# GpSimd's weight low parts in eight instructions, negated maxima on ScalarE, and an earlier window pair and key block, in a hybrid transformer layer on Trainium2

## The chip, the cores and the metric

The kernel runs on one core of one Trainium2 chip. The metric is the device time in microseconds of one execution. A core has five engines that run their own instruction streams and meet at semaphores: TensorE (PE in the profile, with its weight loads shown as PEld), VectorE (DVE), ScalarE (ACT), GpSimd (POOL) and SyncE (SP), which here only issues DMA transfers. Operands lie in on-chip memory (SBUF), matrix products land in PSUM, and everything else is in device memory (DRAM).

## The reference

One layer of a bidirectional trunk: 1024 tokens of width 1024, in three sub-layers. Each of them norms its input, and its normed output is added to the residual.

```python
# 1. mixer: one input projection, then
#    (A) window attention, +-128 tokens, 8 query heads, 2 key/value heads
#    (B) gated delta rule in both directions, 4 heads, chunked
m = jnp.maximum(jnp.max(scores, axis=-1, keepdims=True), sk)      # (A), sk is a sink logit
p = jnp.exp(scores - m)
denom = jnp.sum(p, axis=-1, keepdims=True) + jnp.exp(sk - m)
o = jnp.einsum('bnhgqk,bnkhd->bnqhgd', p / denom, vw)
...
def step(state, inp):                                             # (B), over the chunks
    v_new = u_i - jnp.einsum('bhck,bhkv->bhcv', w_i, state)
    o_i = jnp.einsum('bhck,bhkv->bhcv', qg_i, state) + jnp.einsum('bhij,bhjv->bhiv', qk_i, v_new)
    state = state * gl_i[..., None, None] + jnp.einsum('bhck,bhcv->bhkv', kg_i, v_new)
#    both outputs side by side, times w_out
# 2. cross attention: 4 heads of 256, queries from the tokens (w_cq),
#    keys and values from 256 memory tokens (w_ckv), times w_co
# 3. SwiGLU feed-forward of width 2816
```

## The kernel before

**Products in two parts.** Every float32 operand of a large product is split in a high part, which TensorE takes at full rate, and a low part, which is the rest; a product is then three products (high by high, high by low, low by high). The helper `split` (lines 100 to 106) makes the two: ScalarE copies the source into the high part (line 103), and VectorE, or GpSimd if it is named, subtracts (line 104). Weights go through `load_w` (lines 117 to 129): a 512 KB DMA on SP's queue into `wraw` (line 125), then `split` into `whi` and `wlo`, all from a pool with two buffers each. A weight tile is 128 partitions by 1024 elements, seen as 8 blocks of 128 (`k` = 8) or 2 blocks of 512.

Two callers ask `load_w` for the low part on GpSimd: `next_keys` (lines 976 to 987, a key block: 8 tiles of `w_ckv`, one for each block of 128 columns, 24 products each at line 984 that take `whi` and `wlo` one block of 128 at a time) and `cross_q` (line 1178 on, 16 tiles of `w_cq`, 24 products each at line 276 into `pcq`). Another 12 weight tiles of the feed-forward part have their low part on GpSimd by a call of `split` of their own.

**The middle stage.** Between the input projection (until about 285 us) and the product with `w_out` (from about 536 us) run three kinds of work that don't depend on one another:

- window attention, 16 windows (8 blocks of tokens by 2 key/value heads), by the generator `window` (lines 664 to 722): scores (line 685), scaled and banded scores with their row maximum by VectorE into `sc` and `m4` (line 687), the maximum negated into `nm` (line 692), four exponentials with `nm` as bias on ScalarE (line 694), the sum `es` with the sink (GpSimd 697, ScalarE 698, VectorE 699 and 700), four normalisations (VectorE at 703, ScalarE at 705 for five windows), then transposes (712), a split (`ph`, `pl`), the product with the values (717) and the store into `d_mix`. `next_windows` starts two of them.
- the scan of the gated delta rule by the generator `scan` (lines 825 to 944), 8 steps of four stages for each of two groups. A step is a chain of TensorE products (line 844) and VectorE or ScalarE copies: `kv` (872), `vg` (879), `vn` (881), the state `S` (889 and 892), the outputs `of` and `ol` (900 to 905). In the second half of the steps a gate is applied (919 to 931) and `late` turns, scales (`osq`, line 938) and stores the output into `d_mix` (line 941, SP's queue).
- the cross attention's memory: `memory_norm`, eight `next_keys` and two `next_values`.

The program order of these comes from a list of tokens, `ORDER_3` (line 39), worked off by `issue`: `M` is the memory's norm, `W` a pair of windows, `K` a key block, `V` a half of the values, and `s01` one step of both scans. A scheduler then sets the order on each engine from this program order, from the priorities (`load_w` has a raised one) and from costs of its own. `marks` holds an instruction of each window; the splits of `d_mix` (lines 1147 to 1150), which feed the product with `w_out` at line 1105 (`pmg`), may not be issued ahead of the one of window 14. The first `w_out` tiles go through `load_w` with the low part on VectorE.

Of the kernel before, what the change touches and what calls it, by code (L numbers as in the profile page):

```python
# [14 lines left out]
ALU = mybir.AluOpType  # L15
# [20 lines left out]

ORDER_1 = ("k0 k1 E0 K0 U0 E1 K1 U1 S0 q0 v0 q1 C0 v1 E2 C1 k2 E3 k3 q2 K2 U2 v2 K3 U3 S1 q3 C2 v3 C3 B0 B1").split()
ORDER_2 = "L0 L1 A4 V A0 A1 G0 G1 L2 L3 W W W A2 A3 G2 G3 W".split()
ORDER_3 = ("M s01 W K s01 W K s01 W s01 W K s01 W s01 K K s01 K K K s01 V V s01").split()


_NAMES = ["ident", "mUi", "mLi", "m5", "m6", "band0", "band1", "band2", "mU", "mL", "ones"]
# [34 lines left out]
def tile_hybrid_block(  # L77
# [4 lines left out]
    g_ffn_pre, w_gate_up, w_down, g_ffn_post, consts, out, dump=None, stop=None,  # L82
):
    nc = tc.nc
    x, mem, out = x[0], mem[0], out[0]
# [8 lines left out]
    def f32(ap):  # L94
        return ap.bitcast(F32)
# [4 lines left out]
    def split(hi, lo, src, scale=None, eng=None):  # L100

        if scale is None:
            nc.scalar.copy(hi, src)  # L103
            return (eng or nc.vector).tensor_tensor(lo, src, f32(hi), ALU.subtract)  # L104
        nc.scalar.activation(hi, src, AF.Identity, scale=scale)
        return nc.vector.scalar_tensor_tensor(lo, src, scale, f32(hi), ALU.mult, ALU.subtract)
# [11 lines left out]
    def load_w(src, k, n, eng=None, after=None, place=None):  # L118

        with tc.high_priority(AHEAD):  # L120
            raw = place or wp.tile([P, k, n], F32, tag="wraw", name="wraw")
            with ExitStack() as order_:
                if after:
                    order_.enter_context(tc.issue_after(after.ins))
                nc.sync.dma_start(raw, src.rearrange("(k p) n -> p k n", p=P))
            hi = wp.tile([P, k, n], F32R, tag="whi", name="whi")
            lo = wp.tile([P, k, n], F32R, tag="wlo", name="wlo")
            split(hi, lo, raw, eng=eng)
        return hi, lo


# [47 lines left out]
    sink = prm[:, 16:24]  # L179
# [43 lines left out]
    for hf in range(2):  # L223
        hi = hx.tile([P, KT, HALF], F32R, name=f"hhi{hf}")
        lo = hx.tile([P, KT, HALF], F32R, name=f"hlo{hf}")
# [10 lines left out]
        for k in range(KT):  # L236
# [3 lines left out]
            g = gcol[:, k:k + 1]  # L240
# [89 lines left out]
    for hf in range(2):  # L330
        pp = pg.tile([P, 512], F32, tag="pg", name="pg")
# [331 lines left out]
    def window(n, g):  # L663

        tok = slice(n * P, (n + 1) * P)
        k0, k1 = max(n - 1, 0), min(n + 1, NT - 1) + 1
        nb = k1 - k0
        w = nb * P
        band = C[:, _AT["band0"] - C0 + (k0 - n + 1) * P:][:, 0:w]

        khi, klo = (t[:, k0 * P:k1 * P] for t in keys[g])
        qr = tw.tile([P, 4, P], F32, tag="qr", name="qr", bufs=1)
        for r in range(2):
            nc.sync.dma_start(qr[64 * r:64 * r + 64], d_q[256 * g:256 * g + 256, tok].rearrange("(h e) t -> e h t", h=4))
        qs = tw.tile([P, 4, P], F32R, tag="qs", name="qs")
        nc.scalar.copy(qs, qr)
        nc.gpsimd.tensor_tensor(qs[64:128], qr[64:128], f32(qs[64:128]), ALU.subtract)

        m4 = tw.tile([P, 4], F32, tag="m4", name="m4")
        ssum = tw.tile([P, 4], F32, tag="ssum", name="ssum")  # L680
        pr = []
        for hh in range(4):
            pp = pw.tile([P, 512], F32, tag="pw", name="psw")
            for i, kk in enumerate((khi, klo)):
                nc.tensor.matmul(pp[:, 0:w], qs[:, hh, :], kk, start=(i == 0), stop=(i == 1))
            sc = tw.tile([P, 384], F32, tag="sc", name="sc", bufs=8)
            nc.vector.tensor_tensor_reduce(out=sc[:, 0:w], in0=pp[:, 0:w], in1=band, scale=0.125,
                                           scalar=sink[:, 4 * g + hh:4 * g + hh + 1], op0=ALU.add, op1=ALU.max,
                                           accum_out=m4[:, hh:hh + 1])
            pr.append(sc)  # L690
        nm = tw.tile([P, 4], F32, tag="nm", name="nm")
        turned_round = nc.vector.tensor_scalar(nm, m4, -1.0, None, ALU.mult)
        for hh in range(4):
            nc.scalar.activation(pr[hh][:, 0:w], pr[hh][:, 0:w], AF.Exp, bias=nm[:, hh:hh + 1],
                                 accum_out=ssum[:, hh:hh + 1])
        es = tw.tile([P, 4], F32, tag="es", name="es")
        nc.gpsimd.tensor_tensor(es, sink[:, 4 * g:4 * g + 4], m4, ALU.subtract)
        nc.scalar.activation(es, es, AF.Exp)
        nc.vector.tensor_tensor(es, es, ssum, ALU.add)
        nc.vector.reciprocal(es, es)  # L700
        for hh in range(4):
            if not 8 <= g * NT + n < 13:
                nc.vector.tensor_scalar(pr[hh][:, 0:w], pr[hh][:, 0:w], es[:, hh:hh + 1], None, ALU.mult)
            else:
                nc.scalar.mul(pr[hh][:, 0:w], pr[hh][:, 0:w], es[:, hh:hh + 1])
        marks.append(turned_round)
        yield
        po = pw.tile([P, 4, P], F32, tag="pow", name="pow", bufs=1)
        for j in range(nb):
            pp = pw.tile([P, 512], F32, tag="pw", name="ptw")  # L710
            for hh in range(4):
                nc.tensor.transpose(pp[:, hh * P:(hh + 1) * P], pr[hh][:, j * P:(j + 1) * P], ident)
            ph = tw.tile([P, 512], F32R, tag="ph", name="ph")
            pl = tw.tile([P, 512], F32R, tag="pl", name="pl")
            split(ph, pl, pp)
            for i, pe_ in enumerate((ph, pl)):
                nc.tensor.matmul(po.rearrange("p h t -> p (h t)"), vhl[:, k0 + j, g].rearrange("p r e -> p (r e)"), pe_,
                                 start=(j == 0 and i == 0), stop=(j == nb - 1 and i == 1))
        ao = tw.tile([P, 4, P], F32, tag="ao", name="ao", bufs=1)[0:64]
        nc.scalar.copy(ao, po[64:128])  # L720
        nc.vector.tensor_tensor(ao, po[0:64], ao, ALU.add)
        nc.gpsimd.dma_start(d_mix[g * 256:(g + 1) * 256, tok].rearrange("(h e) t -> e h t", e=64), ao)
# [25 lines left out]
    wins, wins_done, marks = [], [0], []  # L748
# [12 lines left out]
    def issue(order, table):  # L761
        for o in order:
            table[o[0]](*(int(c) for c in o[1:]))
# [245 lines left out]
    def scan_step(pairs):  # L1009

        for _ in range(4):
            for s_ in pairs:
                next(s_, None)

    issue(ORDER_3, {"s": lambda *gs: scan_step([scans[g] for g in gs]), "W": next_windows, "M": memory_norm,
                    "K": next_keys, "V": next_values})
# [126 lines left out]
    for hf in range(2):  # L1143
        for kp in range(4):
            k2 = slice(2 * kp, 2 * kp + 2)
            raw = raws[hf]
# [23 lines left out]
    raw = LR2.enter_context(pool("raw2", 1, side="right")).tile([P, KT, HALF], F32, name="oraw")  # L1170
# [363 lines left out]
    for e in range(EARLY):  # L1534
        f = 2 * e
        w, A = [], []
# [358 lines left out]
```

## Time and profile before

| | |
|---|---|
| median of 3 runs | 1502.69 us |
| the runs | 1501.88, 1502.69 and 1506.23 us |
| profiled execution, its own time | 1504.28 us |
| its span in the trace | 1502.6 us |
| mean granted clock of TensorE | 0.996 of full speed |
| low parts on GpSimd (line 104) | 36, of them 24 by `load_w` |

The span is the stretch from the first to the last recorded instruction; 1.68 us of the execution's time lie around it. A row of the timeline gives the start, the duration, the engine, the line, the operation, the tiles (output, arrow, inputs), shapes, a count, and in square brackets the idle time of that engine just before it with what ended it. A row of the windows view gives a stretch of time, its length, the busy time of PE, PEld, DVE, ACT and POOL in it (with the number of instructions), the granted clock, the busy share of the DMA engines and their rate. A row of the chain of waits gives the start and duration of a piece of the chain of work that ended last.

### The profile page before, as it was taken

The numbers are of one execution on the slowest core, as the hardware profiler recorded it, in microseconds if no ns is written. First come the engines' busy times: TensorE is split into PE (matmuls) and PEld (weight loads), VectorE is DVE, ScalarE is ACT, GpSimd is POOL, SyncE is SP. The second block draws the span as 40 slices with busy tenths as digits, with TensorE's granted clock in tenths as the row PEclk, the third lists the DMA queues.
The fourth block names the chain that finished last, engine by engine and source line by source line (L and its number), as shares of the span: only waits on it lengthen the run. The fifth ranks groups of instructions, "written<-read, shape, count | busy, mean of one in ns | idle before, by whom it ended". The sixth has DMA issues, their size and how long they took to land.

```text
span 1502.6 us, 21339 instructions
## 1 busy us (share of the span) xinstructions
PE 1469.4 (98%) x7437; PEld 1239.6 (82%) x7437; DVE 1109.3 (74%) x1805; ACT 776.2 (52%) x1600; POOL 372.6 (25%) x410
## 2 busy tenths in 40 slices
PE   7999999999999999999999999999999999999998
PEld 6888877888889878888888877888888888888787
DVE  5878998577997866528767887676867764696666
ACT  7678844568467664555654774323223232444533
POOL 0011231442246203242201002343433342000030
PEclk9999999999999999999999999999999999999999
DMA  6244554656996585444855553443533433953355
GB/s 204 71 118 135 138 174 121 174 152 207 317 322 209 155 314 196 153 156 149 275 181 202 182 197 112 127 133 112 165 118 117 140 106 105 350 182 99 105 180 170
DMA packets 254168, 256.35 MB, mean 171 GB/s; under 512 B 18128, under 2 KB 186221, under 8 KB 254061
## 3 DMA queue, kind: packets, MB, share of 16 engines
q1 hardware_dynamic: 252141, 250.80, 52.7%
q0 software_dynamic: 768, 2.10, 0.5%
q10 hardware_dynamic: 1152, 2.10, 0.4%
q8 instruction: 58, 0.95, 0.3%
q14 instruction: 49, 0.40, 0.1%
HBM read 178.63 MB, written 73.70 MB: 168 GB/s over the span
## 4 chain that ended last, share of the span: by engine, by line
PE 68%; DVE 10%; DMA 4%; ACT 4%; issue 3%; SPq 1%; POOL 0%; DVEq 0%; ACTq 0%; POOLq 0%
PE pE L1511 7%; PE pD L1511 7%; PE pmg L1105 6%; PE pcq L276 6%; PE pdX L1733 6%; PE pA L1511 5%; PE pst L1324 5%; PE pB L1511 3%; PE pg L276 3%; PE psc L844 3%; PE pdA L1733 2%; PE pdD L1733 2%; PE pcs L1195 2%; PE pco L1222 1%; PE pck L984 1%
## 5 line engine op out<-in xcount | busy, mean ns | idle before, releaser
L103 ACT CAST whi<-wraw 128x1024 fp32r<-128x1024 f32 x96 | 100.6, 1049 | 123.3 <-DMA wraw<-in_w_gate_up_dram 39.5
L276 PE MATMUL pg<-hlo,whi 128*128 128x512 f32 x352 | 141.0, 401 | 0.0
L276 PE MATMUL pg<-hhi,whi 128*128 128x512 f32 x352 | 140.5, 399 | 0.0
L276 PE MATMUL pg<-hhi,wlo 128*128 128x512 f32 x352 | 140.2, 398 | 0.0
L104 POOL TENSOR_TENSOR wlo<-wraw,whi 128x1024 fp32r<-128x1024 f32 x36 | 88.0, 2444 | 175.8 <-ACT whi L103 163.7
L1511 PE MATMUL pA<-b,whi 128*128 128x512 f32 x352 | 109.8, 393 | 1.9 <-ACT whi L103 1.0
L104 DVE TENSOR_TENSOR wlo<-wraw,whi 128x1024 fp32r<-128x1024 f32 x60 | 74.1, 1235 | 36.1 <-ACT whi L103 31.8
L1511 PEld LDWEIGHTS pA<-b,whi 128*128 128x128 f32 x352 | 65.2, 188 | 17.1 <-ACT whi L103 1.9
L276 PEld LDWEIGHTS pg<-hhi,whi 128*128 128x128 f32 x352 | 67.3, 191 | 13.6 <-ACT hhi L241 0.3
L276 PEld LDWEIGHTS pg<-hhi,wlo 128*128 128x128 f32 x352 | 67.2, 191 | 12.6
L276 PEld LDWEIGHTS pg<-hlo,whi 128*128 128x128 f32 x352 | 67.0, 190 | 12.7
L1733 PE MATMUL pdX<-dhl,whi 128*128 128x512 f32 x264 | 76.1, 390 | 0.9 <-ACT dhl L103 0.7
L1603 POOL TENSOR_TENSOR act<-act,up 128x512 f32<-128x512 f32 x33 | 50.3, 1524 | 88.6 <-DVE up L1602 66.9
L103 ACT CAST whi<-araw 128x1024 fp32r<-128x1024 f32 (+1 forms) x36 | 35.3, 981 | 68.3 <-PE pdX L1733 27.5
L1511 PE MATMUL pA<-b,wlo 128*128 128x512 f32 x176 | 69.0, 392 | 0.5 <-DVE wlo L104 0.5
L104 DVE TENSOR_TENSOR wlo<-araw,whi 128x1024 fp32r<-128x1024 f32 (+1 forms) x36 | 40.7, 1132 | 34.2 <-ACT whi L103 34.1
L1574 POOL TENSOR_TENSOR sr<-wraw 128x512 f32<-128x512 f32 x22 | 29.9, 1357 | 139.8 <-DMA wraw<-in_w_gate_up_dram 86.4
L301 DVE SCALAR_TENSOR_TENSOR acc<-cp,cols,acc 128x1024 f32<-128x1024 f32 x48 | 63.0, 1315 | 0.2
L1733 PEld LDWEIGHTS pdX<-dhl,whi 128*128 128x128 f32 x264 | 49.3, 188 | 12.1 <-ACT dhl L103 1.1
L103 ACT CAST dhl<-b 128x512 fp32r<-128x512 f32 x66 | 40.3, 620 | 31.2 <-PE pdA L1733 13.2
L1575 DVE TENSOR_TENSOR sr<-sr,wraw 128x512 f32<-128x512 f32 x22 | 36.6, 1664 | 26.6 <-POOL sr L1574 26.6
L103 ACT CAST s0h<-sr 128x512 fp32r<-128x512 f32 x22 | 13.7, 622 | 79.3 <-POOL sr L1574 78.9
(504 smaller groups left out, 4330.2 us busy)
## 6 DMA issues: line engine op xcount, KB each, us to landing
wraw<-in_w_gate_up_dram SPq DMA_DIRECT2D x54, 512.0 KB, 3.8
kv<-d_kv SPq DMA_DIRECT2D x32, 512.0 KB, 6.2
wraw<-in_w_in_dram SPq DMA_DIRECT2D x22, 512.0 KB, 4.1
b<-in_w_down_dram SPq DMA_DIRECT2D x20, 512.0 KB, 6.5
araw<-d_as SPq DMA_DIRECT2D x20, 512.0 KB, 3.8
pz<-d_pz SPq DMA_DIRECT2D x32, 256.0 KB, 6.3
wraw<-in_w_ckv_dram SPq DMA_DIRECT2D x16, 512.0 KB, 7.1
wraw<-in_w_out_dram SPq DMA_DIRECT2D x16, 512.0 KB, 4.1
```

Of the source, the lines that this page charges most:

```text
L103: nc.scalar.copy(hi, src)
L104: return (eng or nc.vector).tensor_tensor(lo, src, f32(hi), ALU.subtract)
L276: nc.tensor.matmul(p_, w[:, k, :], ah[a][:, k, :], start=(k == 0 and i == 0), stop=(k == nk - 1 and i == 2))
L301: nc.vector.scalar_tensor_tensor(acc, cp[:, t:t + S], taps[t], acc, ALU.mult, ALU.add)
L844: nc.tensor.matmul(out[:, d, h, :], lt[:, d, h, :], rt[:, d, h, :], start=True, stop=True)
L1105: nc.tensor.matmul(pp[t], act[a][:, k, tt], w_[:, kk, :], start=(k == 0 and i == 0), stop=(k == KT - 1 and i == 2))
L1195: nc.tensor.matmul(pp[:, t2_, :], q[a][:, ct, tt], kr_[b_][:, ct, :], start=(j == 0 and i == 0), stop=(j == 1 and i == 2))
L1324: nc.tensor.matmul(bank, a[:, tt], w, start=(start and i == 0), stop=(stop and i == 2), skip_group_check=not check)
L1511: nc.tensor.matmul(out_, w[a][:, k, :], xx[b_][:, k, :], start=(start and k == 0 and i == 0), stop=(k == HK - 1 and i == 2), skip_group_ch ...
L1575: nc.vector.tensor_tensor(s[1], s[0], a_[:, 0:HK], ALU.subtract)
L1603: nc.gpsimd.tensor_tensor(o_, o_, up, ALU.mult)
L1733: nc.tensor.matmul(banks[t], a[:, k - k0, tt], w, start=(first and k == 0 and i == 0), stop=(k == NB - 1 and i == 2), skip_group_check=not ...
```

## The change

It has three parts. `load_w` with an engine named no longer calls `split`: ScalarE's copy stays one instruction, and the low part becomes eight instructions of 128 by 128 on GpSimd (24 tiles; the 12 of the feed-forward part stay whole). The negated maximum `nm` moves from VectorE to ScalarE, and `marks` holds the last maximum of a window in its place. `ORDER_3` is another: the first pair of windows and the first key block stand ahead of the first scan step, which is then followed by the second one at once, and one of the three key blocks ahead of the eighth step has moved ahead of the pair of windows before the sixth.

```diff
-ORDER_3 = ("M s01 W K s01 W K s01 W s01 W K s01 W s01 K K s01 K K K s01 V V s01").split()
+ORDER_3 = ("M W K s01 s01 W K s01 W s01 W K s01 K W s01 K K s01 K K s01 V V s01").split()
...
-            split(hi, lo, raw, eng=eng)
+            if eng is None:
+                split(hi, lo, raw)
+            else:
+                nc.scalar.copy(hi, raw)
+                for j in range(0, k, 1):
+                    js = slice(j, j + 1)
+                    eng.tensor_tensor(lo[:, js], raw[:, js], f32(hi[:, js]), ALU.subtract)
...
-            nc.vector.tensor_tensor_reduce(out=sc[:, 0:w], in0=pp[:, 0:w], in1=band, scale=0.125,
-                                           scalar=sink[:, 4 * g + hh:4 * g + hh + 1], op0=ALU.add, op1=ALU.max,
-                                           accum_out=m4[:, hh:hh + 1])
+            largest = nc.vector.tensor_tensor_reduce(out=sc[:, 0:w], in0=pp[:, 0:w], in1=band, scale=0.125,
+                                                     scalar=sink[:, 4 * g + hh:4 * g + hh + 1], op0=ALU.add,
+                                                     op1=ALU.max, accum_out=m4[:, hh:hh + 1])
...
-        turned_round = nc.vector.tensor_scalar(nm, m4, -1.0, None, ALU.mult)
+        nc.scalar.mul(nm, m4, -1.0)
...
-        marks.append(turned_round)
+        marks.append(largest)
```

The scheduled order changes with it, from the end of the input projection to the end of the cross attention; the feed-forward part stays as it was. Three places of it follow, by engine, with the line, the operation, the output, an arrow and the inputs. Lines of the changed kernel are six higher than those of before from `load_w` on (line 134 is the new subtraction).

On GpSimd, at the first two key blocks, this is the order before:

```order
L677 TENSOR_TENSOR qs<-qr,qs 64x512
L697 TENSOR_TENSOR es<-prm,m_3468 128x4
L104 TENSOR_TENSOR wlo<-wraw,whi 128x1024
L722 DMA d_mix<-ao 64x4x128
L677 TENSOR_TENSOR qs<-qr,qs 64x512
```

and this is the order now:

```order
L683 TENSOR_TENSOR qs<-qr,qs 64x512
L703 TENSOR_TENSOR es<-prm,m_3468 128x4
L134 TENSOR_TENSOR wlo<-wraw,whi 128x128 x8
L728 DMA d_mix<-ao 64x4x128
L683 TENSOR_TENSOR qs<-qr,qs 64x512
```

The eight small subtractions stand back to back in the place of the large one, with nothing of GpSimd's own between them.

On TensorE, where the scan begins (`psc` are the scan's products, `ptm` the transposes of the memory, `pck` the products of a key block, `psw` and `ptw` the windows' scores and transposes), before:

```order
L969 MATMUL ptm<-ident,mt 128x128 x16
L844 MATMUL psc<-kv,pz 128x128 x3
L685 MATMUL psw<-khi,qs 128x384
L685 MATMUL psw<-klo,qs 128x384
L844 MATMUL psc<-kv,pz 128x128
L712 MATMUL ptw<-ident,sc 128x128 x8
L844 MATMUL psc<-kv,pz 128x128 x2
```

and now:

```order
L691 MATMUL psw<-klo,qs 128x384
L990 MATMUL pck<-mT_4077,whi 128x256
L990 MATMUL pck<-mT_4078,whi 128x256
L850 MATMUL psc<-kv,pz 128x128 x8
L990 MATMUL pck<-mT_4077,wlo 128x256
L990 MATMUL pck<-mT_4077,whi 128x256
```

The first products of the scan have moved behind the start of the first key block, whose other products now lie between them and the next ones of the scan.

On VectorE, at the end of the scans (`osq` is the last output of a group's scan, the rows with `psw` and `m_5099` or `m_5113` are the row maxima of the last window, the last `wlo` is the low part of the first `w_out` tile, those ahead of it are of the values' weights), before:

```order
L703 TENSOR_SCALAR sc<-sc,es 128x384 x4
L938 SCALAR_TENSOR_TENSOR osq<-psc,cols,gate 128x512
L104 TENSOR_TENSOR wlo<-wraw,whi 128x1024
L104 TENSOR_TENSOR pl<-ptw,ph 128x512
L104 TENSOR_TENSOR wlo<-wraw,whi 128x1024
L104 TENSOR_TENSOR pl<-ptw,ph 128x512
L104 TENSOR_TENSOR wlo<-wraw,whi 128x1024
L687 ISA sc,m_5099<-psw,C,prm 128x256
```

and now:

```order
L944 SCALAR_TENSOR_TENSOR osq<-psc,cols,gate 128x512
L693 ISA sc,m_5113<-psw,C,prm 128x256
L693 ISA m_5113 128x1
L104 TENSOR_TENSOR wlo<-wraw,whi 128x1024
L727 TENSOR_TENSOR ao<-pow,ao 64x512
L693 ISA sc,m_5113<-psw,C,prm 128x256
L693 ISA m_5113 128x1
L104 TENSOR_TENSOR wlo<-wraw,whi 128x1024
L693 ISA sc,m_5113<-psw,C,prm 128x256
L693 ISA m_5113 128x1
L104 TENSOR_TENSOR wlo<-wraw,whi 128x1024
```

The last output of the scan no longer stands behind the four normalisations of a window, and all four maxima of the last window (the first of them is just above these rows) stand ahead of `w_out`'s first low part instead of behind it. On SP's queue the load of the first `w_out` tile comes behind two stores of `osq` now, with a load of the values' weights ahead of these, where it came behind four; and the load of the second `w_out` tile comes behind four loads of `d_mix`, where it came behind one.

## The prediction

> **What bounds the kernel now.** I read the page first: the span, the busy times and the shares of the chain that ended last.
>
> ```profile
> span 1502.6 us, 21339 instructions
> PE 1469.4 (98%) x7437; PEld 1239.6 (82%) x7437; DVE 1109.3 (74%) x1805; ACT 776.2 (52%) x1600; POOL 372.6 (25%) x410
> PE 68%; DVE 10%; DMA 4%; ACT 4%; issue 3%; SPq 1%; POOL 0%; DVEq 0%; ACTq 0%; POOLq 0%
> ```
>
> TensorE is busy for 1469.4 of 1502.6 us, and the change removes no product. Only its gaps can be won or widened. Where they lie in the changed part is told by the windows view in stretches of 50 us:
>
> ```profile
> 350.00:400.00 50.00, 46.89 (x336) 42.75 (x336) 39.90 (x104) 34.89 (x81) 12.92 (x15) 1.00 0.90 285
> 400.00:450.00 50.00, 48.35 (x383) 45.67 (x383) 48.12 (x132) 28.74 (x78) 20.70 (x25) 1.00 1.06 319
> 450.00:500.00 50.00, 47.92 (x385) 46.19 (x384) 40.76 (x98) 36.62 (x103) 31.27 (x39) 1.00 0.64 192
> 500.00:550.00 50.00, 48.04 (x242) 40.22 (x241) 38.35 (x75) 31.00 (x71) 5.58 (x12) 0.97 0.74 252
> 550.00:600.00 50.00, 50.00 (x226) 41.46 (x225) 35.35 (x35) 28.79 (x43) 14.20 (x18) 1.00 0.63 212
> ```
>
> TensorE (first busy column) stands still for 3.11 + 1.65 + 2.08 + 1.96 = 8.8 us between 350 and 550, and not at all from 550 on: so the mixing stage can give something, the cross attention only lose. In the mixing stage VectorE is the busiest of the others, 48.12 of 50 us in one stretch. The chain of waits, taken for that stage, shows what the gaps end on:
>
> ```profile
> 374.68 1.72 issue
> 419.88 2.93 DVE sc L703 x4
> 468.44 2.18 DVE nm L692
> 487.71 2.39 DVE es L699
> 526.13 5.42 DMA wraw<-in_w_out_dram
> ```
>
> Three are single VectorE steps that are short elsewhere. The timeline around one of them:
>
> ```profile
> 468.23 2.37 POOL L104 TENSOR_TENSOR wlo<-wraw,whi 128x1024 fp32r<-128x1024 f32 x1
> 468.36 2.27 DVE L692 TENSOR_SCALAR nm<-m 128x4 f32<-128x4 f32 x1
> 470.54 0.68 DVE L879 TENSOR_TENSOR vg<-psc,EG 128x512 f32<-128x512 f32 x1
> 471.27 1.16 PE L844 MATMUL psc<-vg,kv 128*128 128x128 f32 x8 [1.63 <-DVE vg L879]
> L692 DVE TENSOR_SCALAR nm<-m x16: 152/180/2267, 292.1 to 538.6; 128x4 f32<-128x4 f32 x16
> ```
>
> The last row gives `nm`'s durations in ns (least, median, most). An operation on 4 numbers, 180 ns in the median, took 2.27 us here and ended with GpSimd's low part of a key block (468.23 + 2.37 = 470.60); the scan's `vg` came behind it, and TensorE stood still for 1.63 us until that was done. The same happens four more times (below, with the undisturbed form of the four normalisations beside it):
>
> ```profile
> 373.61 3.52 DVE L703 TENSOR_SCALAR sc<-sc,es 128x384 f32<-128x384 f32 x4
> 388.07 1.39 DVE L703 TENSOR_SCALAR sc<-sc,es 128x384 f32<-128x384 f32 x4
> 410.38 1.92 DVE L692 TENSOR_SCALAR nm<-m 128x4 f32<-128x4 f32 x1
> 419.80 3.01 DVE L703 TENSOR_SCALAR sc<-sc,es 128x256 f32<-128x256 f32 x4
> 542.35 1.14 DVE L703 TENSOR_SCALAR sc<-sc,es 128x256 f32<-128x256 f32 x4
> 487.71 2.37 DVE L699 TENSOR_TENSOR es<-es,ssum 128x4 f32<-128x4 f32 x1 [3.02 <-ACT es L698]
> ```
>
> The time held is 2.13, 1.74, 1.87, 2.19 and, above, 2.09 us: 10.0 us of VectorE.
>
> **Term A, eight short subtractions for a long one.** The price of a piece comes from two rows of GpSimd's groups:
>
> ```profile
> L104 POOL TENSOR_TENSOR wlo<-wraw,whi 128x1024 fp32r<-128x1024 f32 x36 | 88.0, 2444 | 175.8 <-ACT whi L103 163.7 <-DMA wpart<-in_w_co_dram 10.2 <-PE pE L1511 1.8
> L921 POOL TENSOR_TENSOR ol<-ol,of 128x256 f32<-128x256 f32 x12 | 8.5, 738 | 8.4 <-DVE ol L905 7.8 <-DVE es L700 0.7
> ```
>
> A line through 1024 elements at 2444 ns and 256 at 738 ns has 2.22 ns an element and 0.17 us fixed, so 0.45 us for 128; the bounds are 0.31 (an eighth of the long one) and 0.74 (no less than the one of twice the size). I take 0.45: 3.63 us for a tile instead of 2.44, 1.2 more, 28 us of GpSimd over 24 tiles. The 175.8 us that GpSimd idles ahead of these subtractions cover that; uncovered it would be 1.2 us for each tile of `cross_q`, 19 us (rival 3). If a held VectorE step gets in when the running piece ends, a hold lasts 0.45 us at most instead of 2.44, and 81% of it goes. What that is worth on TensorE comes from the 10-us stretches in which the holds, or the steps behind them, fall:
>
> ```profile
> 370.00:380.00 10.00, 7.78 (x54) 6.66 (x53) 8.41 (x20) 7.42 (x16) 2.77 (x2) 1.00 1.05 350
> 410.00:420.00 10.00, 8.80 (x66) 7.83 (x66) 10.00 (x22) 6.36 (x17) 4.78 (x5) 1.00 0.97 316
> 470.00:480.00 10.00, 8.73 (x69) 8.44 (x70) 9.22 (x24) 6.52 (x17) 3.79 (x6) 1.00 0.38 112
> 490.00:500.00 10.00, 9.56 (x74) 8.83 (x73) 9.38 (x25) 7.04 (x13) 4.32 (x7) 1.00 0.53 146
> 530.00:540.00 10.00, 8.04 (x33) 6.37 (x32) 7.07 (x15) 8.19 (x12) 0.84 (x2) 0.83 1.02 381
> ```
>
> The first four have 2.22 + 1.20 + 1.27 + 0.44 = 5.1 us of standstill. 81% is **-4.2 us**; the bounds are 0 (other work ends last at these places anyway) and -5.1. I take the near end because four of the holds stand in the chain itself, as rows of their own or as the 1.72 us of "issue" behind the first.
>
> The Trainium skill ("SBUF — State Buffer", section "SBUF: two separate sides") describes the port pair of VectorE and GpSimd as an exclusive lock, kept for a whole instruction, with the other one fully blocked; the row at 468.36 agrees, its 2.27 us ending with GpSimd's 2.37. By that rule the length of one instruction bounds a hold, as taken here; it does not say who gets the pair between two pieces that stand back to back (rival 2).
>
> **Term B, `nm` on ScalarE.** VectorE loses 16 x 0.18 = 2.9 us, in a stage where it is up to 96% busy; ScalarE gains as many operations of the length of its own 128x4 step:
>
> ```profile
> 521.09 0.19 ACT L698 ACTIVATE es<-es 128x4 f32<-128x4 f32 x1
> ```
>
> That is 3.0 us, where ScalarE has 13 to 21 us free in each of the 50-us stretches, and it takes out a hand-over from VectorE to ScalarE for each window. The exponentials had to wait for `nm` before; what queues behind the wait on ScalarE now is what queued behind the first exponential: `ph` and the scan's `vn`. **-0.3**, between -1.5 (half of VectorE's share on the path) and +1.5 (the same on ScalarE's).
>
> **Term C, the order.** The hand-over to `w_out` is in these rows:
>
> ```profile
> 522.40 1.40 DVE L703 TENSOR_SCALAR sc<-sc,es 128x384 f32<-128x384 f32 x4
> 520.25 5.78 SPq L941 DMA_DIRECT2D d_mix<-osq  x4
> 534.42 0.39 PE L685 MATMUL psw<-khi,qs 128*128 128x256 f32 x1 [1.92 <-DVE m L687]
> ```
>
> SP waits in the four stores of `osq` until 526.03 and only then issues the load of `w_out` (526.13, 5.42 us in the chain). The last `osq` follows the four normalisations of 1.40 us, and the last window's scores wait 1.92 us because the maxima stand behind `w_out`'s low part. In the new order neither stands behind the other: the load starts some 1.4 us earlier and the 1.92 go. The stretch from 530 has 1.96 us of standstill, and its clock of 0.83 costs about another 1.4. **-1.8**, down to -3.4 if the clock recovers too. Against it, `w_out`'s second tile comes behind three more loads of 512 KB, of which one was needed for the same products anyway: two at 381 GB/s are 2.75 us. TensorE has 24 products (5.5 us, below) from the first tile, so I put no cost there, and +1.5 as bound. The earlier pair and key block cost nothing in the sum: the order shows key-block products around the scan's first ones, and step two stands where it stood.
>
> **Term D, waits in the cross queries.** Each tile's low part has eight events instead of one, so TensorE gets up to 7 x 24 = 168 more waits.
>
> ```profile
> 650.92 5.50 PE pcq L276 x24
> 1435.30 30.20 PE pdX L1733 x132
> 962.11 2.72 PE pD L1511 x12
> ```
>
> A product takes 229, 229 and 227 ns in these. If the 2 ns in the run of 132 come from its waits, of which the order shows two for 16 products, one is at most 17 ns: 0 to 2.9 us. The first and second row don't differ, with one wait on GpSimd in 24 and one in 8 of any kind, so I take **+0.4**.
>
> Sum: -4.2 - 0.3 - 1.8 + 0.4 = -5.9. On the profiled execution's 1504.28 us (its span of 1502.6 and 1.68 around it) that is 1498.4; that execution lies 1.59 above the median, so on the median 1502.69 - 5.9 = **1496.8 us**.
>
> **Rivals.** 1: *The holds were hidden anyway.* The mixing stage is a bundle of chains, and what VectorE gains the next link (the `kv` loads, GpSimd's own steps) takes back; the order gives nothing. A, B and C shrink to about a quarter: -1.2, or 1501.5. For it: 10.0 us held against 5.1 of standstill. Against it: the 1.63 us that TensorE waits right behind one.
>
> 2: *The pieces don't let VectorE in.* Back to back, the next is there when one ends. A hold then lasts up to 3.63 us, 1.2 more for each of five, of which half (5.1 of 10.0) reaches TensorE: +3.0 instead of -4.2, sum +1.3, or 1504.0. For it: nothing of GpSimd's stands between the pieces. Against it: no row; back-to-back subtractions that read only SBUF, with a step of VectorE between them, aren't in this trace.
>
> 3, on the other side: *GpSimd becomes the bound in `cross_q`.* There TensorE needs 5.50 us a tile, and GpSimd 8 pieces: from 5.50 / 8 = 0.69 us a piece on it sets the pace. At the bound of 0.74 it needs 5.90: 16 x 0.40 = 6.4 us, and the first tile's low part comes 3.5 us later where TensorE has no gap: +9.9. With a piece so long a hold is no shorter in sum, so A is 0: -0.3 - 1.8 + 9.9 + 0.4 = +8.2, or 1510.9. For it: the nearest row by size is that 0.74, and each piece can itself be held by a step of VectorE's. Against it: 1.87 us to spare per tile at 0.45.
>
> 4: *The scan is laid bare at its start.* Steps one and two follow with one key block between them, and one block fewer stands ahead of the last. A step has about three hand-overs like the 1.63 us above; if three come bare, C is +4.9 instead of -1.8: sum +0.8, or 1503.5, worse if more do. Against it: the stretch behind the input projection has key-block products to fill in.
>
> **How the numbers follow.** About 0.3%, 4.5 us, can be told from no change: faster is below 1498.2, slower above 1507.2. The forecast gets 0.56 (its own range is 1493 to 1500; 0.50 of it faster, 0.06 same), rival 1 0.10 (same), rival 2 0.10 (0.06 same, 0.04 slower), rival 3 0.16 (0.15 slower), rival 4 0.08 (0.05 same, 0.03 slower). That gives faster 0.50, same 0.28, slower 0.22. The lowest sum of the bounds is -5.1 - 1.5 - 3.4 = -10.0; more than the 8.8 us of standstill and 1.4 of clock cannot go, which agrees. The highest without rival 3 is 0 + 1.5 + 1.5 + 2.9 = +5.9, 1508.6; with part of rival 3's chance left out, the range is 1492 to 1508.
>
> **What would show it.** Right: no step of VectorE's that ends with GpSimd's subtraction is over about 0.6 us; the pieces average 0.4 to 0.5 us; standstill from 350 to 550 falls from 8.8 to about 3 us; `w_out`'s first load is issued some 1.5 us sooner after the last scan product; from 550 to 850 TensorE stays without gaps. Wrong: VectorE steps of 2 to 4 us beside the pieces (rival 2); holds gone and the standstill as before, now behind `kv` or ScalarE (1); TensorE waiting for `wlo` in `pcq`, pieces over 0.69 us (3); the scan's products waiting in its first two steps (4).

## The result and the profile after

The change makes the kernel a little slower: 1504.24 us in the median of 21 runs (1501.01 to 1508.03) against 1501.26 us (1496.74 to 1507.10) for the kernel before on the same chips. The ratio is 1.0021 with a 95% interval of 1.0012 to 1.0029, so 3 us were lost where 5.9 were forecast to be won. The profiled execution of the changed kernel took 1502.93 us. That is 1.3 below its median, and the profiled execution of before lay 3.0 above its own in these 21 runs: the two spans alone tell nothing, and the comparison goes by stages.

The page of the changed kernel begins:

```profile
span 1501.2 us, 21529 instructions
PE 1467.5 (98%) x7437; PEld 1237.8 (82%) x7437; DVE 1091.6 (73%) x1789; ACT 778.1 (52%) x1616; POOL 401.3 (27%) x578
```

GpSimd has 28.7 us more than before, where 28 were forecast, and VectorE 17.7 us less. TensorE doesn't profit: between 350 and 550 us, where the prediction looked for its standstill to fall from 8.8 to about 3 us, it is 7.8.

The next rows are of the windows view, cut at the events of the program and not at round times: the 30 us behind the last product of the input projection ("start"; that product is issued at 361.15 us before, since the projection runs beside the first windows from 286 us on and does not end at 285 us, as the description of the kernel has it), from there to 8 us before the last product of the values ("middle"), from there to 16 us behind the first product with `w_out` ("hand-over"), and the rest of that product up to the cross queries. First before, then the changed kernel:

```profile
361.10:391.10 30.00, 26.89 (x196) 24.28 (x196) 25.29 (x66) 21.33 (x48) 6.78 (x7) 1.00 1.03 334
391.10:523.70 132.60, 128.87 (x973) 121.12 (x972) 117.58 (x295) 86.87 (x241) 61.01 (x75) 1.00 0.79 238
523.70:552.30 28.60, 26.64 (x125) 21.78 (x124) 18.73 (x34) 15.91 (x28) 0.84 (x2) 0.94 0.94 333
552.30:632.20 79.90, 79.90 (x371) 66.48 (x370) 49.47 (x54) 42.54 (x69) 18.61 (x24) 1.00 0.51 167
```

```profile
358.40:388.40 30.00, 26.27 (x179) 23.51 (x178) 23.41 (x61) 21.29 (x49) 11.59 (x23) 0.94 1.00 317
388.40:522.00 133.60, 132.57 (x1004) 125.03 (x1003) 114.39 (x296) 88.25 (x251) 66.68 (x116) 1.00 0.77 240
522.00:551.40 29.40, 26.33 (x116) 20.84 (x116) 19.18 (x27) 19.54 (x32) 1.53 (x3) 0.94 1.01 360
551.40:629.90 78.50, 78.50 (x365) 65.31 (x364) 46.46 (x51) 38.84 (x65) 18.78 (x30) 1.00 0.48 159
```

What TensorE loses in a stretch is its length less its busy time, and the share of the length that the granted clock (third number from the end) lacks. Before: 3.1 at the start, 3.7 in the middle, 2.0 + 1.7 at the hand-over. Changed: 3.7 + 1.8, then 1.0, then 3.1 + 1.8. The gain in the middle is there; the start and the hand-over take it back.

A second profile of each kernel (the last two experiments) shows which of this belongs to the kernel and which to one execution. Before, then changed:

```profile
359.40:389.40 30.00, 26.86 (x197) 24.30 (x196) 25.32 (x66) 21.38 (x48) 6.77 (x7) 1.00 1.02 332
389.40:521.40 132.00, 128.86 (x972) 121.12 (x971) 115.38 (x295) 86.88 (x241) 61.83 (x75) 1.00 0.77 239
521.40:549.10 27.70, 26.40 (x127) 21.07 (x126) 19.49 (x35) 16.50 (x29) 0.84 (x2) 1.00 0.95 334
```

```profile
356.90:386.90 30.00, 26.26 (x178) 23.47 (x178) 23.25 (x61) 21.32 (x49) 11.31 (x23) 0.94 1.00 309
386.90:520.80 133.90, 132.57 (x1005) 125.00 (x1004) 114.65 (x297) 88.55 (x251) 67.01 (x117) 1.00 0.76 241
520.80:550.70 29.90, 26.50 (x119) 21.10 (x118) 18.22 (x27) 18.61 (x31) 1.54 (x3) 0.94 1.01 358
```

The changed kernel repeats itself to 0.3 us in every stretch. Before has 3.1, 3.1 and 1.3 now: the 1.7 us of lost clock at its hand-over, which the prediction had put into the lower bound of term C, was not there again. From the first window product to the first feed-forward product the two profiles of before took 569.4 and 567.9 us, those of the changed kernel 570.1 and 570.9, 1.9 more in the mean. That much of the measured 3 us has a place. The feed-forward products up to the last at line 1511, whose order is the same in both, took 427.1 us in both profiles of before and 428.3 and 428.1 in those of the changed kernel. But in the profiles of the other kernels below they took from 427.0 to 428.7, and 428.2 in the kernel before with nothing but some casts held back, so these 1.1 us can't be told from the spread of single executions. Where the rest of the 3 us lies stays open.

### The profile page after: what moved, and what is told of

Its sections match the earlier page's. It is cut to its first block, busy times and chain, and to the rows that moved or that the text cites. A ratio compares the mean times of both kernels' runs of the same rounds, so it can differ in the third digit from the quotient of the medians.

```text
span 1501.2 us, 21529 instructions
## 1 busy us (share of the span) xinstructions
PE 1467.5 (98%) x7437; PEld 1237.8 (82%) x7437; DVE 1091.6 (73%) x1789; ACT 778.1 (52%) x1616; POOL 401.3 (27%) x578
## 5 line engine op out<-in xcount | busy, mean ns | idle before, releaser
L103 ACT CAST whi<-wraw 128x1024 fp32r<-128x1024 f32 x72 | 75.5, 1050 | 98.2 <-DMA wraw<-in_w_gate_up_dram 39.5
L134 POOL TENSOR_TENSOR wlo<-wraw,whi 128x128 fp32r<-128x128 f32 x192 | 89.3, 501 | 98.7 <-ACT whi L131 93.8
L103 ACT CAST dhl<-b 128x512 fp32r<-128x512 f32 x66 | 40.3, 619 | 31.4 <-PE pdA L1739 13.3
L1517 PE MATMUL pB<-s0h,s1h 128*128 128x512 f32 x176 | 54.3, 390 | 0.9 <-ACT s1h L103 0.9
```

The source lines that it names most:

```text
L134: eng.tensor_tensor(lo[:, js], raw[:, js], f32(hi[:, js]), ALU.subtract)
L1517: nc.tensor.matmul(out_, w[a][:, k, :], xx[b_][:, k, :], start=(start and k == 0 and i == 0), stop=(k == HK - 1 and i == 2), skip_group_ch ...
```

## The experiments

The runs were to tell theories apart. Theory 1: the pieces earn what was forecast, and the new list gives it back. Theory 2: the pieces themselves cost. Theory 3: `nm` costs on ScalarE. Theories 4 and 5, on the stretch behind the hand-over, came up on the way.

**The three parts one by one, and the pieces with `nm`.** The list alone:

```diff
-ORDER_3 = ("M s01 W K s01 W K s01 W s01 W K s01 W s01 K K s01 K K K s01 V V s01").split()
+ORDER_3 = ("M W K s01 s01 W K s01 W s01 W K s01 K W s01 K K s01 K K s01 V V s01").split()
```

> The kernel before with the new list of tokens alone (large low parts, nm on VectorE). Theory 1 (the order gives back what the pieces earn): slower than before by 4 to 7 us, with 3 us or more of TensorE standstill between 360 and 372 us, where the scan's first products no longer fill the wait for the windows' softmax, and a half-clock stretch behind it. Theory 2 (the pieces cost, the order is neutral): within 2 us of before.

The pieces alone (the change's edit of `load_w`), and `nm` alone (its edit of `window`):

> The kernel before with the eight pieces alone. Theory 1: faster than before by 2 to 4 us, no VectorE step of over 1 us beside a piece, standstill between 350 and 550 us down from 8.8 to about 5. Theory 2: slower than before by 2 to 4 us, though the holds are gone, because of GpSimd's 28 us more and TensorE's 168 waits.

> The kernel before with nm on ScalarE alone. Theory 1 and 2: within 1.5 us of before. Theory 3 (the hand-over on ScalarE costs, since nm queues behind copies of the weights' high parts): slower by 2 to 4 us, with TensorE waiting longer for ph.

Both of these, with the old list:

> The changed kernel with the old list of tokens (pieces and nm on ScalarE). Theory 1: faster than before by 2 to 4 us, so some 5 to 7 us faster than the changed kernel. Theory 2: as slow as the changed kernel, 2 to 4 us above before. Theory 3: slower than the pieces alone by 2 to 4 us.

| kernel | median, us | ratio to before, interval | start | middle | hand-over | rest of `w_out` |
|---|---|---|---|---|---|---|
| list | 1504.24 | 1.0013 (1.0000 to 1.0026) | 6.4 | 1.4 | 4.9 | 0 |
| pieces | 1505.21 | 1.0024 (1.0011 to 1.0038) | 1.1 | 3.2 | 9.4 | 0 |
| `nm` | 1507.33 | 1.0046 (1.0029 to 1.0063) | 3.5 | 2.8 | 2.0 | 6.8 |
| pieces and `nm` | 1506.33 | 1.0034 (1.0018 to 1.0050) | 3.9 | 2.6 | 1.2 | 7.6 |

The last four columns are TensorE's loss as above, from one profile of each kernel. No theory foresaw all of this. Every part alone is slower than before (1502.08 in these runs): the list by 2.2 us and hardly clear of the noise, where theory 1 had 4 to 7; the pieces by 3.1, as theory 2 had it; `nm` by 5.3, more than the 2 to 4 of theory 3. `nm`, and pieces with `nm`, lose 7 us in a stretch in which the kernel before loses nothing; the pieces alone lose 9.4 us at the hand-over, 5.0 of them in the clock. TensorE's longest waits there end on the windows' `ph` (1.27 and 1.57 us) and maxima (1.15); why these come late was not followed further.

The first thing that the table settles is term A. With the list alone the low parts are whole, VectorE is still held by them, and yet the middle loses 1.4 us instead of 3.7. VectorE's timeline of that kernel, and its middle stretch:

```profile
395.12 3.31 DVE L703 TENSOR_SCALAR sc<-sc,es 128x384 f32<-128x384 f32 x4
411.47 2.38 DVE L703 TENSOR_SCALAR sc<-sc,es 128x256 f32<-128x256 f32 x4
```

```profile
387.30:520.90 133.60, 132.18 (x998) 124.41 (x998) 115.75 (x301) 86.06 (x241) 61.11 (x74) 1.00 0.76 238
```

With pieces and `nm` and the old list VectorE is hardly held any more, and the middle still loses 2.6. The second row is its longest wait in that stretch:

```profile
385.90:517.20 131.30, 128.73 (x967) 121.22 (x966) 108.17 (x280) 87.86 (x244) 68.94 (x124) 1.00 0.78 241
411.76 0.50 PE L723 MATMUL pow<-ph,vhl 128*128 128x512 f32 x1 [1.10 <-ACT ph L103]
```

Counted alike in all profiles between 280 and 560 us (what `nm`, `es` and the normalisations take over 0.3 us more than undisturbed), VectorE is held for 12.3 us before (9.5 in the second profile), 9.3 with the list, 4.5 with the pieces, 3.6 with `nm`, 1.2 with pieces and `nm`, 3.2 in the changed kernel. The middle loses 3.7 (3.1), 1.4, 3.2, 2.8, 2.6 and 1.0: it follows the list, and hardly the holds. (In the run with pieces, `nm` and the hold on the casts that follows, VectorE is held for 1.2 us and the middle loses 4.0.)

**The casts of `d_mix` (theory 4).** The loss behind the first products with `w_out` has its cause on ScalarE. In the kernel with pieces and `nm`, with the old list (the numbers in square brackets are the idle time and what ended it):

```profile
564.53 1.05 ACT L103 CAST b<-b 128x1024 fp32r<-128x1024 f32 x1 [7.51 <-DMA b<-d_mix]
568.74 1.04 ACT L103 CAST b<-b 128x1024 fp32r<-128x1024 f32 x1 [3.17 <-DMA b<-d_mix]
569.69 1.04 ACT L103 CAST whi<-wraw 128x1024 fp32r<-128x1024 f32 x1
570.78 0.79 PE L1111 MATMUL pmg<-whi,s0h 128*128 128x512 f32 x1 [4.07 <-ACT whi L103]
559.86 0.62 POOL L728 DMA_DIRECT2D d_mix<-ao  x1 [9.05 <-DVE ao L727]
```

The casts of the second half of `d_mix` (tile `b`) wait for their loads, and these, but for the first, for the store of the last window, issued at 559.86. ScalarE takes its instructions in program order here: it sits idle for 3.17 us ahead of the second of these casts, with the cast of the seventh `w_out` tile behind it, whose load had been issued by 558.40 and landed 4.8 us later. Two of the casts stand ahead of that tile's, and TensorE waits 4.07 us for it. The kernel before has one such cast there, the first, whose load went out at 559.86, ahead of the last window's store at 563.63. The edit queues the casts behind the eighth `w_out` tile:

```diff
-    for hf in range(2):
+    def load_half(hf, after):
...
-            with tc.issue_after(marks[14].ins):
+            with tc.issue_after(after.ins):
                 split(mxT[hf][0][:, k2, :], mxT[hf][1][:, k2, :], raw[:, k2, :])
+
+    load_half(0, marks[14])
     LR.close()
     xn0 = mid_gemm(tz, mxT[0], w_out, gp, x, d_x1, 0, banks=([PG] * 4, [PX] * 2 + [PN] * 2), vec=True)
+    load_half(1, casts[7])
```

(`casts` holds ScalarE's copies of the weight tiles of that product.)

> The pieces and nm on ScalarE with the old list of tokens, and the casts of the second half of d_mix queued on ScalarE behind the eighth w_out weight cast (before they stood around the seventh). Theory 4 (those casts wait for the last window and hold the seventh weight tile): the stretch from the first w_out product to the first cross query falls from 103 to 95 to 97 us, the time by 5 to 7 us against the run without the hold, to about 1500, 1 to 3 us under before. Theory 5 (the standstill only moves, since the second half's products wait for the same stores): the stretch stays over 100 us and the time within 2 us of the run without the hold.

As a control the same hold in the kernel before:

> The kernel before with the same hold on the casts of d_mix's second half, as a control. Theory 4: the kernel before has one of these casts ahead of the seventh weight cast and loses nothing there, so within 2 us of before, the w_out stretch 94 to 97 us. If the hold is worth something by itself, 3 us or more faster.

With pieces and `nm` the hold took the median from 1506.33 to 1500.74 us, a ratio to before of 0.9993 (0.9983 to 1.0004) instead of 1.0034, and the stretch from the first `w_out` product to the first cross query from 103.3 to 97.7 us (97 at most was expected). The control measured 1501.92, 0.9997 (0.9981 to 1.0014), with 95.3 us in that stretch against 95.9. Theory 4 is shown; theory 5 falls.

The changed kernel does not have this loss, though its order has all four of the casts ahead of the seventh weight tile. ScalarE and GpSimd there:

```profile
554.06 0.62 POOL L728 DMA_DIRECT2D d_mix<-ao  x1 [8.32 <-DVE ao L727]
562.52 3.18 ACT L103 CAST b<-b 128x1024 fp32r<-128x1024 f32 x3
566.97 1.05 ACT L103 CAST b<-b 128x1024 fp32r<-128x1024 f32 x1 [1.27 <-DMA b<-d_mix]
568.45 1.05 ACT L103 CAST whi<-wraw 128x1024 fp32r<-128x1024 f32 x1 [0.43 <-DMA wraw<-in_w_out_dram]
```

Its last window is stored 18.6 us after the first `w_out` product (535.44), against 31.4 in the kernel above, so the casts find their data. That is what the new order of the last window's maxima bought; its price is at the hand-over, below.

**Which half of the list.** First the moved key block without the early pair, then the early pair and key block without the moved one, then the early pair with the first scan step ahead of the key block; all with pieces and `nm`:

```diff
-ORDER_3 = ("M W K s01 s01 W K s01 W s01 W K s01 K W s01 K K s01 K K s01 V V s01").split()
+ORDER_3 = ("M s01 W K s01 W K s01 W s01 W K s01 K W s01 K K s01 K K s01 V V s01").split()
...
+ORDER_3 = ("M W K s01 s01 W K s01 W s01 W K s01 W s01 K K s01 K K K s01 V V s01").split()
...
+ORDER_3 = ("M W s01 K s01 W K s01 W s01 W K s01 K W s01 K K s01 K K s01 V V s01").split()
```

> The changed kernel with its list of tokens half undone: the first scan step is back ahead of the first pair and key block, the key block stays moved to ahead of the sixth step's pair. Theory 1 (the early pair and key block lay the start of the scan bare): the mixing stage is 248 to 250 us instead of 252, without the 3.5 us of standstill between 360 and 370. Rival (the moved key block lays the end bare): it stays at 251 to 253. The whole time follows only if the w_out stretch stays near 95 us; over 100 it is as slow as the pieces with the old list.

> The changed kernel with only the early pair and key block in its list, the three key blocks ahead of the eighth step as before. Theory 1: the mixing stage is as long as the changed kernel's or longer, 251 to 254 us, with over 3 us of standstill in the first 12 us behind the last input projection product. Rival: 248 to 250 us.

> The changed kernel with the first scan step between the early pair and the early key block. Standstill plus clock loss in the first 30 us behind the input projection is 5.4 to 6.4 us in every kernel with pair and key block ahead of the first step, 1.1 to 4.6 in every other. If the pair ahead of the scan's first products makes it (TensorE's order is fixed, and the pair waits for its softmax), it stays over 5 here; if the key block does, it is 3 to 4.5 and the time 2 us under the changed kernel's.

They measured 1506.38 (1.0035, 1.0019 to 1.0051), 1503.68 (1.0009, 0.9995 to 1.0023) and 1508.24 us (1.0041, 1.0027 to 1.0055). The start loses 4.1, 5.4 and 3.9 us, the middle 1.8, 1.3 and 2.0. The mixing stage, from the first window product to the first with `w_out`, took 245.7, 248.7 and 247.3 us, against 252.2 in the changed kernel; the first and the third then lost 7.0 and 5.5 us to the casts as above. So the pair alone does not lay the start bare, the pair with the key block does. The second expectation was missed on the whole stage: the early pair and key block lose 5.4 us at the start, but the stage came out 3.5 us shorter than the changed kernel's. That is no gain: the product with `w_out` and what lies between its products, up to the first cross query, took 98.7 us there and 94.5 in the changed kernel, so that the two stretches together are 347.4 and 346.7. The third kernel's time was expected 2 us under the changed kernel's and came out 2.9 over it (1505.39 in the same runs), by the casts.

**The other combinations.** The new list with the pieces (`nm` on VectorE), the new list with `nm` (low parts whole), the moved key block with pieces, `nm` and the hold, and the moved key block with the hold alone:

> The new list and the pieces, nm on VectorE. If the 1.0 us of standstill left in the middle of the mixing stage of the changed kernel is owed to the list and not to the pieces, it is 1 to 2 us here too, as with the list alone (1.4). Start: 3 us or more of standstill and a half-clock stretch behind it, as in each kernel with the early pair. Time 1503 to 1507.

> The new list and nm on ScalarE, low parts whole: the changed kernel without the pieces. If the pieces earn nothing in the mixing stage: 251 to 252 us there, VectorE held for 4 us or more in sum, yet a standstill in the middle of 1 to 2 us; time within 2 us of the changed kernel's. If the pieces earn what was forecast: middle standstill 4 us or more, time 1507 to 1509.

> The pieces, nm on ScalarE, the list with the moved key block alone (first scan step ahead of the first pair), and the hold on the casts of d_mix's second half. Theory (the early pair costs the start, the casts ahead of the seventh weight tile cost the w_out stretch, and both are undone here): mixing stage 245 to 248 us, w_out stretch 95 to 98, time 1496 to 1499, faster than both kernels by 3 to 7 us. Rival (whatever one stage gains the next takes back): 1500 to 1503.

> The kernel before with the moved key block and the hold alone, low parts whole and nm on VectorE. If the pieces and nm matter in the best combination: mixing stage 249 to 251 us and 1500 to 1502. If the list does it alone: 245 to 248 and 1496 to 1499.

| kernel | median, us | ratio to before, interval | start | middle | hand-over | rest of `w_out` |
|---|---|---|---|---|---|---|
| list, pieces | 1508.64 | 1.0057 (1.0045 to 1.0069) | 6.4 | 2.1 | 2.3 | 5.4 |
| list, `nm` | 1504.97 | 1.0027 (1.0018 to 1.0035) | 5.5 | 1.8 | 4.8 | 0 |
| key block, pieces, `nm`, hold | 1500.64 | 0.9997 (0.9985 to 1.0008) | 3.9 | 2.0 | 6.4 | 0.1 |
| key block, hold | 1504.06 | 1.0023 (1.0010 to 1.0035) | 3.1 | 3.0 | 2.6 | 0 |

The 5.4 us of the first row are another wait than the casts: TensorE stands 3.73 us ahead of a window's product until the one before it is out of PSUM (`ao`, VectorE). The list with `nm` is within 1 us of the changed kernel: in the new list the pieces earn nothing that can be measured. With the moved key block alone the middle loses 2.0 us with pieces and `nm` (third row) and 3.0 without (fourth), so there about 1 us may be theirs, by one profile each. The third was meant to beat both kernels and is only as fast as before: it beats the changed kernel, but what it won in the middle went at the hand-over, as its rival said. The fourth stays open: its one profile is of an execution of 1499.17 us, its median is 1504.06.

**Both kernels again**, unedited, for the second profiles above:

> The changed kernel unchanged, a second profile. If the account by stages holds: 5 to 6.5 us lost at the start with a half-clock stretch near 370 us, 1 to 2 in the middle, 4 to 5 at the hand-over to w_out, none behind it; the stretch from the first window product to the feed-forward part 569.5 to 572 us.

> The kernel before unchanged, a second profile. If the account by stages holds: 3 to 4.6 us lost at the start, 3 to 4 in the middle, 1 to 4 at the hand-over, the stretch from the first window product to the feed-forward part 568 to 570 us, so 1.5 to 2.5 under the changed kernel's.

They measured 1505.39 (1.0029, 1.0018 to 1.0041) and 1500.11 us (0.9992, 0.9977 to 1.0006).

## Why the prediction was wrong

**Term A** (-4.2 forecast). Its mechanism held. A piece costs 0.46 us in the median, 0.50 in the mean, where 0.45 was taken, and in this kernel VectorE gets in between the pieces, so rival 2's price falls. GpSimd's pieces (least, median and most in ns):

```profile
L134 POOL TENSOR_TENSOR wlo<-wraw,whi x192: 448/461/1444, 370.8 to 738.5; 128x128 fp32r<-128x128 f32 x192
```

and from the timeline a run of eight of them with four steps of VectorE's beside it, and the longest hold that is left, 1.1 us over the normal time where it was up to 2.2; it stands beside two of the scan's steps on GpSimd, and not beside a piece:

```profile
396.26 3.75 POOL L134 TENSOR_TENSOR wlo<-wraw,whi 128x128 fp32r<-128x128 f32 x8 [4.88 <-ACT whi L131]
395.98 2.03 DVE L709 TENSOR_SCALAR sc<-sc,es 128x384 f32<-128x384 f32 x4
462.22 1.29 DVE L705 TENSOR_TENSOR es<-es,ssum 128x4 f32<-128x4 f32 x1
462.04 1.44 POOL L927 TENSOR_TENSOR ol<-ol,of 128x256 f32<-128x256 f32 x2
```

The Trainium skill ("SBUF — State Buffer", section "SBUF: two separate sides") has the pair of ports locked for a whole instruction and leaves open who comes next. The trace agrees: VectorE's normalisations from 395.98 on took 0.64 us over their normal time beside pieces of 0.46, where a whole low part had cost them 2.13. That VectorE comes next is no rule, though. In the kernel with the new list, the pieces and `nm` on VectorE, one step on 4 numbers was held until a run of eight pieces had ended (473.31 + 3.39 = 476.70), as rival 2 has it:

```profile
473.31 3.39 POOL L134 TENSOR_TENSOR wlo<-wraw,whi 128x128 fp32r<-128x128 f32 x8
474.75 1.96 DVE L705 TENSOR_TENSOR es<-es,ssum 128x4 f32<-128x4 f32 x1
```

In the ten profiles with pieces no other step was held over more than two of them; what sets this one apart is not known.

The step that failed is the conversion of a hold into a gain: "81% is -4.2 us", which took all of TensorE's standstill in the four stretches for the holds' doing. With the old list the middle keeps 2.6 to 4.0 us when the holds are mostly gone, and with pieces and `nm` its longest wait is for ScalarE's `ph` (1.10 us, above), where before it was for the scan's `vg` behind a held `nm` (1.63); with the new list it has 1.4 when they are not. A row in the chain that ends last shows who was last there, not how far ahead the next one was. That is rival 1's mechanism and its sign (the holds gone, a standstill behind ScalarE), with another cause, the list, for the gain in the middle.

**Term B** (-0.3). With `nm` alone the mixing stage didn't get longer (248.9 us against 250.2 and 249.2 in the two profiles of before). But with the old list the reshuffled order put two casts of `d_mix` (with the pieces) or three (`nm` alone) ahead of the seventh weight tile, where before has one, and `nm` alone became the slowest single part. The term's bounds were drawn from the operation's length; the cost came from the order that the scheduler made around it.

**Term C** (-1.8). Two of its steps failed. The first is "the earlier pair and key block cost nothing in the sum". TensorE's rows at the start of the changed kernel, its four longest waits and the scan's first products:

```profile
363.12 0.66 PE L718 MATMUL ptw<-ident,sc 128*128 128x128 f32 x4 [0.63 <-DVE m L693]
364.10 0.50 PE L723 MATMUL pow<-ph,vhl 128*128 128x512 f32 x1 [0.32 <-ACT ph L103]
367.85 0.44 PE L691 MATMUL psw<-khi,qs 128*128 128x384 f32 x1 [0.72 <-DVE m L693]
369.79 0.49 PE L723 MATMUL pow<-ph,vhl 128*128 128x512 f32 x1 [1.32 <-ACT ph L103]
372.18 2.65 PE L850 MATMUL psc<-kv,pz 128*128 128x128 f32 x16
```

and the scan's products of the kernel before that lay between the same window products:

```profile
364.27 0.83 PE L844 MATMUL psc<-kv,pz 128*128 128x128 f32 x6
366.99 0.61 PE L844 MATMUL psc<-kv,pz 128*128 128x128 f32 x4
367.80 1.05 PE L844 MATMUL psc<-vg,kv 128*128 128x128 f32 x8
```

Before, the scan's first products were issued into the waits of the windows. Now they stand behind the pair, TensorE has only windows for 10 us, and each wait for a softmax is bare. What put them there is the key block in the list: in the run with the first scan step between the pair and the key block, the scan's first eight products are issued at 358.27, ahead of 12 of the memory's transposes, and the start loses 3.9. The prediction looked at key-block products around the scan's first ones, and not at what stood ahead of them. That is rival 4's mechanism, one place earlier than it was put. Behind the standstill the clock is low as well: all five kernels with pair and key block ahead of the first step lose 5.4 to 6.4 us at the start, 1.8 to 3.3 of it in the clock; the others, 1.1 to 4.6. (The 4.6 are those of the control with the hold, whose order at the start is that of before; it lost 1.8 of them in the clock, so the cost of the new start has a spread of that size.)

The second is "neither stands behind the other". The load of the first `w_out` tile, expected 1.4 us sooner, was issued 4.3 and 3.8 us after the scan's last product in the two profiles, against 3.9 in both of before. The wait of 1.92 us is gone, but the last window's softmax moved into the gap:

```profile
528.69 0.20 ACT L698 ACTIVATE nm<-m 128x4 f32<-128x4 f32 x1 [1.70 <-DVE m L693]
528.80 1.03 ACT L103 CAST whi<-wraw 128x1024 fp32r<-128x1024 f32 x1
529.84 0.49 ACT L700 ACTIVATE sc<-sc,nm 128x256 f32<-128x256 f32 x1
531.93 0.58 ACT L103 CAST ph<-ptw 128x512 fp32r<-128x512 f32 x1
532.35 1.14 DVE L709 TENSOR_SCALAR sc<-sc,es 128x256 f32<-128x256 f32 x4
533.40 0.68 DVE L104 TENSOR_TENSOR pl<-ptw,ph 128x512 fp32r<-128x512 f32 x1
532.57 0.51 PE L723 MATMUL pow<-ph,vhl 128*128 128x512 f32 x1 [1.71 <-ACT ph L103]
534.14 0.80 PE L723 MATMUL pow<-pl,vhl 128*128 128x512 f32 x1 [1.07 <-DVE pl L104]
535.44 0.78 PE L1111 MATMUL pmg<-whi,s0h 128*128 128x512 f32 x1
```

The last window's four exponentials (the first is at 529.84) wait behind a weight cast of 1.03 us. On ScalarE they stand ahead of the `ph` of the window before, and on VectorE the four normalisations that follow from them stand ahead of its `pl`. TensorE waits 1.71 and 1.07 us for these two, and the first product with `w_out` stands behind them; the first `w_out` tile itself was cast by 529.83. The hand-over loses 4.9 and 5.2 us in the two profiles, against 3.7 and 1.3 before. This is read from the trace, and no run undid it; the list alone loses 4.9 there too. So the changed kernel has about +2.4 at the start, +2.5 at the hand-over and -2.3 in the middle against before, and the list alone +3.3, +2.4 and -2.0 by one profile, where -1.8 stood in the sum for the order.

**Term D** (+0.4). The cross queries took 117.1 and 117.0 us with the pieces and 117.8 without, the rest of the cross attention 106.4 against 105.6: +0.1 in all, TensorE without a gap. Rival 3 did not come about, though single pieces are held up by VectorE's steps (1.44 us at most, in the row of the pieces above); the 168 waits cost nothing that shows.

**The base.** The sum was set on a median of three runs, 1502.69 us, which 21 runs put at 1501.26. Its gaps were read from one execution that lay 3 us above the latter, with a low clock at the hand-over that the second profile does not have.

## What to carry over

A step that is held, stands in the chain of waits and has an idle TensorE behind it is still only worth the distance to the next reason for that idleness; ask what would be last if it were gone, and count only that. In a kernel whose order a scheduler makes anew, an edit of one operation costs or earns more by the order that comes out (here up to 7 us) than by its own duration: compare the queues of the in-order engines at the next hand-over, and look for an instruction that waits on late data ahead of one that is ready. Take two profiles of the kernel before, if a term of the sum is a gap of 2 us in one.

## What was not expected of the hardware

Short waits bring the clock down too. In the changed kernel TensorE was busy for 65% of the ten us ahead, with no single wait over 1.32 us, and the ten us behind them were granted 0.83:

```profile
360.00:370.00 10.00, 6.50 (x39) 4.58 (x37) 7.37 (x20) 9.68 (x25) 2.17 (x3) 1.00 0.90 260
370.00:380.00 10.00, 9.77 (x68) 9.39 (x68) 7.25 (x16) 6.51 (x15) 5.88 (x11) 0.83 1.06 357
```

The kernel with the new list alone shows the same with no wait over 1.14 us, though TensorE was busy for 79% of the ten us ahead:

```profile
356.00:366.00 10.00, 7.86 (x48) 6.18 (x46) 9.07 (x22) 8.35 (x18) 2.16 (x3) 1.00 0.76 221
366.00:376.00 10.00, 9.06 (x46) 8.09 (x46) 8.44 (x18) 6.52 (x16) 3.60 (x3) 0.66 1.05 351
```

The kernel before, busy for 78% of ten us (370 to 380), kept 1.00. So the busy share of ten us does not tell when the clock falls, and no limit can be read from these runs. The Trainium skill ("TensorE: Matmul & The Clock Gate", Part 1 on the clock gate) gives half rate after an idle window of about 3.4 us. The 0.17 of 10 us that the changed kernel lost is what 3.4 us at half rate cost, which agrees in length; but here the idleness was made of waits of which none came near that length.
